# Norms between layers moved to VectorE in two halves with plain transposes, and a longer chunk-wise end of the feed-forward's last product

## The chip, the cores and the metric

The kernel runs on one core of a Trainium2 chip. The metric is the device time of one launch in microseconds (us). Each kernel is run several times; one execution is also recorded by the hardware profiler. The engines are named as in the profile: PE (TensorE, matrix products), PEld (its weight loads), DVE (VectorE), ACT (ScalarE), POOL (GpSimd) and SP (SyncE, which issues the weight transfers).

## The reference, cut to what matters

A block with adaptive norms, a Fourier and windowed-attention mixer and a mixture of experts is followed by a two-layer model. All tensors are float32, the sequence has 512 tokens and the width is 1024. The second model:

```python
def rms_norm(x, g):
    y = xf * lax.rsqrt(jnp.mean(xf * xf, axis=-1, keepdims=True) + NORM_EPS)
    return y * g

def conv_ffn(h, w_up, conv_w, conv_b, w_down):      # widths 1024 -> 2*2816 -> 1024
    u = causal_dwconv(h @ w_up, conv_w, conv_b)
    gate, up = jnp.split(u, 2, axis=-1)
    return (jax.nn.silu(gate) * up) @ w_down

x = first_block(...)                                 # phases A and B
for i in range(2):
    h = rms_norm(x, pre_g[i])                        # i = 0: even mixer, phase C
    h = mixer(h, ...)                                # i = 1: odd mixer, phase E
    x = x + rms_norm(h, post_g[i])
    h = conv_ffn(rms_norm(x, ffn_pre_g[i]), ...)     # phases D and F
    x = x + rms_norm(h, ffn_post_g[i])
```

So there are four norms of the whole x between layers: before C, before D, before E and before F.

## The kernel before, in words

The 512 tokens are four chunks of 128 rows; x stays in SBUF as four tiles of 128 x 1024. A product needs its left side transposed (hT, eight blocks of 128 columns of the width by 512 tokens). To keep float32 accuracy every operand is split into a high and a low part, and each product is three matmuls (mm3, lines 381 to 385: hi*hi, hi*lo, lo*hi). Weights arrive as float32 pieces through SP (L344), ACT casts the high part (L373), DVE subtracts to get the low part (L374); the two parts lie in rings of three buffers each (pool wp).

Phases run in the order A (first mixer), B (experts), C (even mixer), D (feed-forward 0), E (odd mixer), F (feed-forward 1). Each transition has the same steps, chunk by chunk. The last product of a phase is run by proj_m: with tail = n, the weight pieces of the last n*step blocks are held back and then used chunk by chunk, so that chunk 0 is finished early; evac takes a finished chunk from PSUM, and with a lag of one chunk post_norm (L456 to L460) adds the normed result to x, and the norm for the next phase follows. In feed-forward phases evac adds to osb (L1727), sums the squares on ACT (L414) and multiplies by the post gain on POOL (L1729); tail is 2 for the second half of the width of the last product. Blocks are counted by 128 of the inner width, 11 for this product, and step is 2; so with tail 2 the last two weight pieces (three blocks) are used chunk by chunk.

The norm (normer, L443 to L454) of one chunk: POOL multiplies x by the gain (L449, 128x1024), ACT sums squares (L414), ACT and DVE form the reciprocal root (rstd, L391 to L405), DVE writes a 128x128 diagonal of it (L452), and PE multiplies each of eight 128x128 blocks of the result by that diagonal, which transposes and scales at once (L438). ACT and DVE split each group of four blocks out of PSUM into the high and low part of hT (L388, L389). In B the scatter of the last two experts (L1172) and the add to x (L1175) are run chunk by chunk in front of the norm.

The order on each engine is made when the kernel is built: a scheduler takes instructions by their place in the program and by when their inputs are ready in its own model; an instruction that is pinned keeps its place. Within an engine the order is fixed at run time, so one that waits holds up those behind it. A row of gains (gain, L1249; row_load, L324) comes by a POOL-queue DMA that is pinned. In out_proj (L1437) the gain of the next norm is asked for before the post gain is loaded and scaled on POOL (L1441).

At the end of F no norm follows: store_chunk writes x out.

Of the kernel before, what the change touches and what calls it, by code (L numbers as in the profile page):

```python
# [9 lines left out]
F32 = mybir.dt.float32  # L10
# [5 lines left out]
OP = mybir.AluOpType  # L16
# [5 lines left out]
D = 1024  # L22
# [5 lines left out]
NF = DFF // 128  # L28
# [4 lines left out]
ROUTE = ((), (0,), (0, 1), (0, 1, 2, 3, 1, 2, 3, 2, 3))  # L33
SIDE = ()
NFIRST = 4
FILL = (0, 2, 2, 3, 3, 2, 2, 2, 0, 0, 0)
ODD = ("v0 v1 d0 d0 d0 d0 d0 d0 d0 d0 s0 d1 s0 d1 s0 d1 d0 d1 d1 s0 d1 s1 s0 d1 d1 s1 d1 s1 s1 s1").split()

# [24 lines left out]
def weight_chunks(phase):  # L63
# [6 lines left out]
    if phase == "A":  # L70
# [12 lines left out]
        for h in range(2):  # L83
            add("q", 2048, lambda z, h=h: _m(z["w_in"][0][:, qcols], 4 * h, 4, 0, 512))
            if h == 0:
                ada(3)
                ada(1)
            fill(FILL[h])
        add("kv", 2048, lambda z: _m(z["w_in"][0], 0, 8, 1024, 256))
        fill(FILL[2])  # L90
        for j in range(2):
            add("u", 2048, lambda z, j=j: _s(z["w_in"][0], slice(j * 256, j * 256 + 256)))
            fill(FILL[3 + j])
        for i in range(4):
            fill(FILL[5 + i])
        orow = np.array(list(range(512)) + [512 + (kv * 4 + r) * 64 + d for r in range(4) for kv in range(2)
                                            for d in range(64)])
        for half in range(2):
            for h in range(2):
                add("o", 2048, lambda z, h=h, half=half: _m(z["w_out"][0][orow], 4 * h, 4, half * 512, 512))  # L100
                if half:
                    fill(FILL[9 + h])
    if phase == "B":
# [160 lines left out]
class Kernel:  # L264
# [160 lines left out]
        nc.vector.scalar_tensor_tensor(out, xg, r, shift, op0=OP.mult, op1=OP.add)  # L425
        return out

    def transpose_split(self, rows, c, hT, bank=None, diag=None):

        nc = self.nc  # L430
        for g in range(2):
            pt = (bank or self.av)()
            for k in range(4):
                kk = 4 * g + k
                if diag is None:
                    nc.tensor.transpose(pt[:, k * 128:(k + 1) * 128], rows[:, kk * 128:(kk + 1) * 128], self.ident)
                else:
                    nc.tensor.matmul(pt[:, k * 128:(k + 1) * 128], rows[:, kk * 128:(kk + 1) * 128], diag,  # L438
                                     start=True, stop=True)
            dst = [h[:, 4 * g:4 * g + 4, c * 128:(c + 1) * 128] for h in hT]  # L440
            self.split(dst[0], dst[1], pt.rearrange("p (k t) -> p k t", k=4))

    def normer(self, gain, hT, bank=None):  # L443

        nc = self.nc

        def norm(c):
            xg = self.nrm.tile([128, D], F32, name="xn", tag="xn")
            nc.gpsimd.tensor_tensor(xg, self.x[:, c], gain, op=OP.mult)  # L449
            r = self.rstd(self.ssq(self.x[:, c]), 1, D)  # L450
            diag = self.sp.tile([128, 128], F32, name="diag", bufs=2)
            nc.vector.tensor_scalar(diag, self.ident, r, -0.5, op0=OP.mult, op1=OP.mult)  # L452
            self.transpose_split(xg, c, hT, bank, diag)
        return norm  # L454

    def post_norm(self, c, og, s0, s1):  # L456
# [549 lines left out]
    def phase_b(self, er, ep, after):  # L1006
# [5 lines left out]
        for i in range(2 + NRAW):  # L1012
            if i == 2 + NFIRST:
                self.pin(nc.sync.dma_start(self.hd[384:], self.last))
            ins = self.fetch(self.pos + i, *((self.wp, 2) if i < 2 else (pc, NRAW)))
            if i >= 2 + NFIRST:
                self.pin(ins)
# [660 lines left out]
    def phase_ffn(self, l, hT, after):  # L1678
        nc, tc, sp = self.nc, self.tc, self.sp
        with ExitStack() as es:  # L1680
            p = self.pool(es, "f_p")
            post = self.row_load(p, "ffn_post", D, l * D)
            nc.gpsimd.tensor_scalar(post, post, -0.5, None, op0=OP.mult)
            os_ = p.tile([128, 4, D], F32, name="osb")
            aT = self.pair_tile(p, "aT", 11)

            def gated(j, pss):
                u = []
# [15 lines left out]
            for si, (a, b) in enumerate(SEGS):  # L1704
                for j in range(a, b):
                    ws = self.pieces("up", 128)
                    if j == 0:
                        pss = [self.mm(), self.mm()]
                        self.proj_first(hT, list(ws), pss)
                    else:  # L1710
                        pss = []
                        for w in ws:
                            pss.append(self.mm())
                            self.proj_s(hT, w, pss[-1])
                    gated(j, pss)
                if si:
                    self.table()
                    nxt = after(p)
                for half in range(2):
                    sl = slice(half * 512, half * 512 + 512)  # L1720

                    def evac(c, ps):
                        o = os_[:, c, sl]
                        if si == 0:
                            nc.scalar.copy(o, ps)
                            return
                        nc.vector.tensor_tensor(o, o, ps, op=OP.add)  # L1727
                        s = self.ssq(o)
                        nc.gpsimd.tensor_tensor(o, o, post[:, sl], op=OP.mult)  # L1729
                        if half == 0:  # L1730
                            first[c] = self.half_sum(s)
                        else:
                            return lambda: (self.post_norm(c, os_[:, c], first[c], s), nxt(c))
                    self.proj_m(aT, "down", 3, 11, 512, evac, banks=[self.av] * 2 + [self.tp] * 2, tail=2 * half * si)

    def store_chunk(self, c):
        self.nc.sync.dma_start(self.out[c * 128:(c + 1) * 128], self.x[:, c])
# [53 lines left out]
```

## Time and profile before

| what | value |
|---|---|
| median of 3 runs | 2146.18 us (2145.84 to 2146.59) |
| the profiled execution's own time | 2144.74 us |
| its span, first to last instruction | 2143.0 us |
| PE busy | 2019.7 us (94%) |
| DVE busy | 1365.0 us (64%) |
| ACT busy | 1054.7 us (49%) |
| POOL busy | 186.5 us (9%) |
| mean granted TensorE clock | 0.980 |

Busy shares are averages over phases. What the change touches lies in five short stretches: around 857 to 880 us (B to C), 1109 to 1137 (C to D), 1490 to 1523 (D to E), 1742 to 1770 (E to F) and the last 20 us. In such a stretch the idle time of PE and the instruction that ends it tell more than the shares. [...]

### The profile page before, as it was taken

To read this page: it belongs to the slowest core of one execution; us is meant where nothing else is said; L and a number is where in the kernel's file an instruction comes from. 1 tells how busy PE (TensorE), PEld (TensorE's weight loads), DVE (VectorE), ACT (ScalarE), POOL (GpSimd) and SP (SyncE) were. 2 spreads that over 40 slices of the span, in tenths; PEclk is the share of its full clock that TensorE was granted. 3 is DMA by queue.
4 is the path that set the end of the run, shared out by engine and by line. 5 is a ranking of instruction groups with operands and counts; after the bars stand their busy time and mean duration, and the time that the engine had idled before them with its cause. 6 is when DMAs were issued, how large, how long until landed. Compare 5 with 4: busy or idle time off the path is not lost.

```text
span 2143.0 us, 25155 instructions
## 1 busy us (share of the span) xinstructions
PE 2019.7 (94%) x9459; PEld 1576.9 (74%) x9459; DVE 1365.0 (64%) x2304; ACT 1054.7 (49%) x1826; POOL 186.5 (9%) x166
## 2 busy tenths in 40 slices
PE   6899789999999999999999999999999999999997
PEld 5667667766666666877778888887887778888886
DVE  7675579988888888627755533553436766534553
ACT  3344277767676776426644433443325554423432
POOL 2103400000000000300011000002200030000002
PEclk8899889999999999999999999999999999999999
DMA  7744669999999995320122222222321022222221
GB/s 285 203 156 174 281 214 365 387 341 345 351 339 343 345 356 211 102 89 30 40 79 99 99 88 99 98 90 79 110 89 60 24 85 99 99 89 98 99 83 65
DMA packets 53933, 358.32 MB, mean 167 GB/s; under 512 B 6694, under 2 KB 7262, under 8 KB 14004
## 3 DMA queue, kind: packets, MB, share of 16 engines
q1 hardware_dynamic: 48148, 338.60, 42.6%
q0 software_dynamic: 5664, 18.12, 3.2%
q8 instruction: 74, 1.21, 0.2%
q14 instruction: 47, 0.39, 0.1%
HBM read 353.28 MB, written 4.46 MB: 167 GB/s over the span
## 4 chain that ended last, share of the span: by engine, by line
PE 83%; DVE 10%; ACT 3%; DMA 2%; issue 2%; POOL 0%; SPq 0%; DVEq 0%; ACTq 0%; POOLq 0%
PE mm L1098 14%; PE mm L384 13%; PE mm L383 13%; PE mm L385 13%; PE mm L1095 4%; DVE wlo L374 3%; PE tp L1128 2%; PE av L1172 2%; PE av L385 2%; PE av L383 2%; PE av L384 2%; PE tp L383 2%; PE tp L385 2%; PE tp L384 2%; PE mm L1223 1%
## 5 line engine op out<-in xcount | busy, mean ns | idle before, releaser
L374 DVE TENSOR_TENSOR wlo<-wraw,whi 128x1024 fp32r<-128x1024 f32 (+1 forms) x545 | 648.5, 1216 | 470.2 <-ACT whi L373 469.5
L373 ACT CAST whi<-wraw 128x1024 fp32r<-128x1024 f32 (+1 forms) x545 | 548.8, 1044 | 415.0 <-PE mm L384 151.9
L383 PE MATMUL mm<-hT_hi,whi 128*128 128x512 f32 (+1 forms) x960 | 374.8, 392 | 4.7 <-ACT whi L373 4.5
L384 PE MATMUL mm<-hT_lo,whi 128*128 128x512 f32 (+1 forms) x960 | 374.5, 390 | 2.2 <-DVE hT_lo L389 2.2
L385 PE MATMUL mm<-hT_hi,wlo 128*128 128x512 f32 (+1 forms) x960 | 373.4, 389 | 0.0
L383 PEld LDWEIGHTS mm<-hT_hi,whi 128*128 128x128 f32 x960 | 181.0, 189 | 47.2 <-ACT whi L373 5.3
L384 PEld LDWEIGHTS mm<-hT_lo,whi 128*128 128x128 f32 x960 | 181.2, 189 | 43.6 <-DVE hT_lo L389 3.0
L385 PEld LDWEIGHTS mm<-hT_hi,wlo 128*128 128x128 f32 x960 | 181.0, 189 | 40.8
L1098 PE MATMUL mm<-wlo,xs 128*128 128x512 f32 x448 | 164.1, 418 | 7.7 <-DVE wlo L374 7.6
L1098 PE MATMUL mm<-whi,xs 128*128 128x512 f32 x448 | 170.0, 428 | 0.4 <-ACT whi L373 0.4
L383 PE MATMUL mm<-whi,hT_hi 128*128 128x512 f32 (+2 forms) x288 | 110.6, 386 | 0.0
L384 PE MATMUL mm<-wlo,hT_hi 128*128 128x512 f32 (+2 forms) x288 | 110.1, 383 | 0.3 <-DVE wlo L374 0.3
L385 PE MATMUL mm<-whi,hT_lo 128*128 128x512 f32 (+2 forms) x288 | 109.2, 381 | 0.0
L1098 PEld LDWEIGHTS mm<-wlo,xs 128*128 128x128 f32 x448 | 77.7, 190 | 42.0 <-DVE wlo L374 28.4
L1098 PEld LDWEIGHTS mm<-whi,xs 128*128 128x128 f32 x448 | 83.4, 190 | 26.5 <-issue 8.4
L1172 PE MATMUL av<-y,ph 128*128 128x512 f32 x256 | 84.9, 427 | 14.1 <-ACT y L388 11.3
L1729 POOL TENSOR_TENSOR osb<-osb,row_ffn_post 128x512 f32<-128x512 f32 x16 | 25.4, 1599 | 708.8 <-ACT junk L414 379.1
L388 ACT CAST aT_hi<-cv 128x512 fp32r<-128x512 f32 x44 | 27.3, 621 | 118.9 <-DVE cv L1700 117.0
L1098 PE MATMUL mm<-wlo,act 128*128 128x512 f32 x224 | 81.0, 424 | 3.7 <-DVE wlo L374 3.6
L1098 PE MATMUL mm<-whi,act 128*128 128x512 f32 x224 | 81.7, 427 | 0.0
L1172 PEld LDWEIGHTS av<-y,ph 128*128 128x128 f32 x256 | 48.6, 192 | 40.9 <-ACT y L388 21.7
L1699 ACT ACTIVATE cv<-cv 128x512 f32<-128x512 f32 x44 | 27.8, 633 | 89.6 <-DVE cv L1696 89.6
(484 smaller groups left out, 3414.8 us busy)
## 6 DMA issues: line engine op xcount, KB each, us to landing
wraw<-in_wts SPq DMA_DIRECT2D x310, 1024.0 KB, 5.5
wraw<-in_wts SPq DMA_DIRECT2D x8, 768.0 KB, 4.3
x<-in_x SPq DMA_DIRECT2D x4, 512.0 KB, 11.1
out<-x SPq DMA_DIRECT2D x4, 512.0 KB, 2.6
wraw<-in_wts SPq DMA_DIRECT2D x2, 832.0 KB, 6.2
bias<-t5scr POOLq DMA_DIRECT2D x8, 192.0 KB, 15.8
hd<-xn POOLq DMA_DIRECT2D x3, 512.0 KB, 3.6
mod<-md POOLq DMA_DIRECT2D x1, 1024.0 KB, 11.0
```

What stands on the lines that cost most here:

```text
L373: i1 = nc.scalar.copy(hi[:, :n], t[:, a:a + n])
L374: i2 = nc.vector.tensor_tensor(lo[:, :n], t[:, a:a + n], hi[:, :n].bitcast(F32), op=OP.subtract)
L383: mm(ps, a[0], b[0], start=start, stop=False)
L384: mm(ps, a[0], b[1], start=False, stop=False)
L385: mm(ps, a[1], b[0], start=False, stop=stop)
L388: self.nc.scalar.copy(hi, src)
L1095: nc.tensor.matmul(ps[half], full[:, WHOLE.index(k)], w[:, sl], start=(k == 0), stop=(k == 7))
L1098: nc.tensor.matmul(ps[half], stat[:, k], w[q][:, 0, sl], start=(k + q == 0), stop=(k == 7 and q == 1))
L1128: nc.tensor.matmul(pt[:, k * 128:(k + 1) * 128], src[:, f * 128:(f + 1) * 128], dup, start=True, stop=True)
L1172: nc.tensor.matmul(ps, ph[:, c * 128:(c + 1) * 128], y[:, q, sl], start=(n == 1), stop=(n == 2 * len(es)))
L1699: nc.scalar.activation(u[0], u[0], AF.Silu)
L1729: nc.gpsimd.tensor_tensor(o, o, post[:, sl], op=OP.mult)
```

## The change: what it does, and the diff

In normer the gain row is multiplied by -0.5 once (on POOL); a chunk's norm then has, for each half of the width, one DVE instruction x * r * gain of 128x512, and four plain transposes on PE against the constant identity, and the split. The POOL product, the diagonal and the products with it are gone. In the feed-forward phases the tail constant of the last product's second half goes from 2 to 4 (seven of its eleven blocks are run chunk by chunk, from four held pieces), the weight parts of these phases go round five buffers instead of three (two more of each in the phase's own pool), and the post gain of the second half is multiplied on DVE.

```diff
--- before.py
+++ after.py
@@ -33,6 +33,7 @@
 ROUTE = ((), (0,), (0, 1), (0, 1, 2, 3, 1, 2, 3, 2, 3))
 SIDE = ()
 NFIRST = 4
+TAIL = 4
 FILL = (0, 2, 2, 3, 3, 2, 2, 2, 0, 0, 0)
 ODD = ("v0 v1 d0 d0 d0 d0 d0 d0 d0 d0 s0 d1 s0 d1 s0 d1 d0 d1 d1 s0 d1 s1 s0 d1 d1 s1 d1 s1 s1 s1").split()
 
@@ -425,32 +426,28 @@
         nc.vector.scalar_tensor_tensor(out, xg, r, shift, op0=OP.mult, op1=OP.add)
         return out
 
-    def transpose_split(self, rows, c, hT, bank=None, diag=None):
+    def transpose_split(self, rows, c, hT, g, bank=None):
 
         nc = self.nc
-        for g in range(2):
-            pt = (bank or self.av)()
-            for k in range(4):
-                kk = 4 * g + k
-                if diag is None:
-                    nc.tensor.transpose(pt[:, k * 128:(k + 1) * 128], rows[:, kk * 128:(kk + 1) * 128], self.ident)
-                else:
-                    nc.tensor.matmul(pt[:, k * 128:(k + 1) * 128], rows[:, kk * 128:(kk + 1) * 128], diag,
-                                     start=True, stop=True)
-            dst = [h[:, 4 * g:4 * g + 4, c * 128:(c + 1) * 128] for h in hT]
-            self.split(dst[0], dst[1], pt.rearrange("p (k t) -> p k t", k=4))
+        pt = (bank or self.av)()
+        for k in range(4):
+            kk = 4 * g + k
+            nc.tensor.transpose(pt[:, k * 128:(k + 1) * 128], rows[:, kk * 128:(kk + 1) * 128], self.ident)
+        dst = [h[:, 4 * g:4 * g + 4, c * 128:(c + 1) * 128] for h in hT]
+        self.split(dst[0], dst[1], pt.rearrange("p (k t) -> p k t", k=4))
 
     def normer(self, gain, hT, bank=None):
 
         nc = self.nc
+        nc.gpsimd.tensor_scalar(gain, gain, -0.5, None, op0=OP.mult)
 
         def norm(c):
+            r = self.rstd(self.ssq(self.x[:, c]), 1, D)
             xg = self.nrm.tile([128, D], F32, name="xn", tag="xn")
-            nc.gpsimd.tensor_tensor(xg, self.x[:, c], gain, op=OP.mult)
-            r = self.rstd(self.ssq(self.x[:, c]), 1, D)
-            diag = self.sp.tile([128, 128], F32, name="diag", bufs=2)
-            nc.vector.tensor_scalar(diag, self.ident, r, -0.5, op0=OP.mult, op1=OP.mult)
-            self.transpose_split(xg, c, hT, bank, diag)
+            for g in range(2):
+                sl = slice(g * 512, g * 512 + 512)
+                nc.vector.scalar_tensor_tensor(xg[:, sl], self.x[:, c, sl], r, gain[:, sl], op0=OP.mult, op1=OP.mult)
+                self.transpose_split(xg, c, hT, g, bank)
         return norm
 
     def post_norm(self, c, og, s0, s1):
@@ -1683,6 +1680,7 @@
             nc.gpsimd.tensor_scalar(post, post, -0.5, None, op0=OP.mult)
             os_ = p.tile([128, 4, D], F32, name="osb")
             aT = self.pair_tile(p, "aT", 11)
+            self.parts = (([(self.wp, 3)] * 3 + [(p, 2)] * 2) * 14)[:2 * NF + 24]
 
             def gated(j, pss):
                 u = []
@@ -1726,12 +1724,12 @@
                             return
                         nc.vector.tensor_tensor(o, o, ps, op=OP.add)
                         s = self.ssq(o)
-                        nc.gpsimd.tensor_tensor(o, o, post[:, sl], op=OP.mult)
+                        (nc.vector if half else nc.gpsimd).tensor_tensor(o, o, post[:, sl], op=OP.mult)
                         if half == 0:
                             first[c] = self.half_sum(s)
                         else:
                             return lambda: (self.post_norm(c, os_[:, c], first[c], s), nxt(c))
-                    self.proj_m(aT, "down", 3, 11, 512, evac, banks=[self.av] * 2 + [self.tp] * 2, tail=2 * half * si)
+                    self.proj_m(aT, "down", 3, 11, 512, evac, banks=[self.av] * 2 + [self.tp] * 2, tail=TAIL * half * si)
 
     def store_chunk(self, c):
         self.nc.sync.dma_start(self.out[c * 128:(c + 1) * 128], self.x[:, c])
```

## Rows read from the trace of the kernel before

**Rows 1.** Page of the profile: chain of work that ended last, shares by engine.

```profile
PE 83%; DVE 10%; ACT 3%; DMA 2%; issue 2%; POOL 0%; SPq 0%; DVEq 0%; ACTq 0%; POOLq 0%
```

**Rows 2.** Windows: stretch, length, busy us (instructions) by engine, clock, DMA share, GB/s.

```profile
857.00:877.00 20.00, 17.03 (x91) 13.74 (x90) 17.17 (x38) 9.88 (x24) 13.48 (x9) 0.91 0.27 78
977.00:1003.00 26.00, 25.99 (x153) 20.06 (x152) 19.75 (x89) 18.55 (x58) 0.54 (x1) 1.00 0.05 11
1109.00:1137.00 28.00, 23.52 (x176) 21.34 (x175) 18.78 (x41) 14.45 (x33) 11.49 (x7) 1.00 0.22 71
1140.00:1490.00 350.00, 350.00 (x1498) 281.52 (x1497) 168.90 (x198) 130.44 (x171) 5.95 (x4) 1.00 0.27 94
1490.00:1500.00 10.00, 5.90 (x26) 4.42 (x24) 7.91 (x13) 6.16 (x16) 7.92 (x4) 0.94 0.05 7
1500.00:1510.00 10.00, 8.46 (x38) 7.44 (x39) 7.61 (x16) 3.61 (x10) 3.69 (x2) 0.72 0.25 101
1742.00:1770.00 28.00, 23.54 (x167) 21.70 (x166) 17.49 (x39) 14.13 (x32) 10.80 (x6) 0.94 0.16 57
```

**Rows 3.** Timeline of PE at boundaries: start, length, instructions, idle before and its releaser.

```profile
865.27 0.50 PE L1172 MATMUL av<-y,ph 128*128 128x512 f32 x1 [1.96 <-DVE x L1175]
...
1128.54 2.02 PE L438 MATMUL av<-diag,xn 128*128 128x128 f32 x16 [1.81 <-DVE diag L452]
...
1500.57 3.76 PE L438 MATMUL av<-diag,xn 128*128 128x128 f32 x16 [4.67 <-DVE diag L452]
...
1508.98 2.02 PE L438 MATMUL av<-diag,xn 128*128 128x128 f32 x16 [0.97 <-DVE rs_y L404]
...
1761.39 3.51 PE L438 MATMUL av<-diag,xn 128*128 128x128 f32 x16 [1.83 <-DVE diag L452]
```

**Rows 4.** Groups by form, 1195 to 2143 us: count, busy us, mean ns, idle before.

```profile
L438 PE MATMUL av<-diag,xn 128*128 128x128 f32 x128 | 19.4, 315 | 9.0 <-DVE diag L452 8.0 <-DVE rs_y L404 1.0
...
L1641 PE MATMUL tp<-ident,s 128*128 128x128 f32 x32 | 4.5, 274 | 0.0
...
L452 DVE TENSOR_SCALAR diag<-ident,rs_y 128x128 f32<-128x128 f32 x8 | 2.4, 294 | 0.1
...
L1700 DVE TENSOR_TENSOR cv<-cv,cv 128x512 f32<-128x512 f32 x39 | 27.0, 692 | 1.4
```

**Rows 5.** Timeline of DVE: instructions beside POOL work, and the same ones without.

```profile
862.21 2.41 DVE L404 SCALAR_TENSOR_TENSOR rs_y<-rs_t,rs_y 128x1 f32<-128x1 f32 x1
...
1498.70 1.21 DVE L400 SCALAR_TENSOR_TENSOR rs_t<-rs_y,rs_v 128x1 f32<-128x1 f32 x1
...
1501.48 0.21 DVE L400 SCALAR_TENSOR_TENSOR rs_t<-rs_y,rs_v 128x1 f32<-128x1 f32 x1
...
1530.05 1.23 DVE L374 TENSOR_TENSOR wlo<-wraw,whi 128x1024 fp32r<-128x1024 f32 x1 [3.91 <-ACT whi L373]
...
1729.41 2.06 DVE L374 TENSOR_TENSOR wlo<-wraw,whi 128x1024 fp32r<-128x1024 f32 x1 [0.38 <-ACT whi L373]
```

**Rows 6.** Timelines of POOL and DVE where POOL scales a row of gains.

```profile
871.56 0.54 POOL L327 DMA_DIRECT2D row_lq<-in_rows  x1 [0.88 <-ACT hT_hi L388]
...
875.46 1.23 POOL L1274 TENSOR_SCALAR row_cq<-row_cq 128x384 f32<-128x384 f32 x1
...
1729.36 2.77 POOL L1441 TENSOR_SCALAR row_od_post<-row_od_post 128x1024 f32<-128x1024 f32 x1 [4.49 <-DMA row_od_post<-in_rows]
...
1732.16 1.89 DVE L1449 TENSOR_TENSOR osb<-mm,row_od_post 128x512 f32<-128x512 f32 x3 [0.69 <-POOL row_od_post L1441]
```

**Rows 7.** Timelines of PE, DVE and POOL at the kernel's end.

```profile
2129.68 0.40 PE L385 MATMUL tp<-whi,aT_lo 128*128 128x512 f32 x1
...
2132.39 0.68 DVE L1727 TENSOR_TENSOR osb<-osb,tp 128x512 f32<-128x512 f32 x1
...
2136.53 1.28 DVE L460 SCALAR_TENSOR_TENSOR x<-osb,rs_y,x 128x1024 f32<-128x1024 f32 x1
...
2133.89 2.32 POOL L1729 TENSOR_TENSOR osb<-osb,row_ffn_post 128x512 f32<-128x512 f32 x1 [2.51 <-ACT junk L414]
```

## The prediction

> **What bounds the kernel now.** I read the page's chain first: TensorE carries 83% of it, VectorE 10% [rows 1]. So a microsecond is won where TensorE works less or waits less. Then I asked for windows, to see where it waits. In the body of a feed-forward phase it is busy 350 of 350 us at full clock, in the stretch 1140 to 1490 [rows 2] (phase F looks the same). Nothing done to casts or buffers there can bring anything. The boundaries are different: idle time of TensorE is 2.97 us at B to C (20 less 17.03), 4.48 at C to D, 4.10 and 1.54 in the two stretches of D to E, 4.46 at E to F [rows 2]. The granted clock falls with it: 0.91, 1.00, 0.94 and 0.72, 0.94. Third, the timeline of TensorE at these places says who ends the wait [rows 3]: nearly always the norm (diag, rs_y), once, at B to C, the add to x. Fourth, the timeline of VectorE shows small instructions that last 2.41 and 1.21 us where 0.21 is usual, each beside a POOL product [rows 5]. Last, the end: after its last product the kernel runs a chain of VectorE, ScalarE and POOL [rows 7].
>
> **The change part by part.** The profiled execution took 2144.74 us (span 2143.0 and 1.74 around it), 1.44 under the median of the runs, 2146.18. Gains are worked out in its timeline and taken off the median.
>
> *Plain transposes.* A chunk's norm now issues 16 records on TensorE for its eight products with the diagonal, 2.02 us at full clock [rows 3]; a product of two plain float32 operands counts twice. The attention phases do the same 128x128 transposes against the identity with one record each, 32 in 4.5 us, 0.14 each [rows 4]; eight are 1.13. That is 0.89 us less per chunk, 3.6 per boundary, 14.2 for sixteen chunks. It is worth that only where TensorE is the limit.
>
> *Two halves on VectorE.* The diagonal (0.29) goes and two instructions of 128x512 with two SBUF inputs come; the nearest row is 0.69 [rows 4]. So VectorE has 1.09 more per chunk, and it no longer shares time with the POOL product: up to 1.0 back per chunk (1.21 against 0.21 [rows 5]). The chain from the reciprocal root to the first transposed half was 0.29 and half of 2.02, 1.30; it becomes 0.69 and half of 1.13, 1.25. To the second half it was 2.31 and becomes 1.94. So the chain of a chunk is between 0 and 0.4 shorter.
>
> *C to D and E to F.* There the last wait is for the norm (1.81 and 1.83 before the fourth chunk [rows 3]), which stands behind ScalarE's sum of squares and VectorE's splits. The shorter TensorE work turns into idle time, the chain gains up to 0.4 per chunk (1.5 in all), the heavier VectorE queue may lose as much. I take 0 for each, bounds 1.5 either way.
>
> *B to C.* The wait of 1.96 for x [rows 3] comes from a VectorE instruction of 2.41 beside POOL [rows 5]; without it 2.0 are won. TensorE could save 3.6 more, but VectorE is busy 17.17 of 20 here [rows 2] and gets 4.4 more, against 2.2 and 1.0 of blocked time that go. Bounds: 5.6 won to 1 lost. I take 2.5, near the one wait that has a row.
>
> *D to E, the longer chunk-wise end.* Now the last product runs three of eleven blocks by chunks, so the chunks end close together, and TensorE has nothing before the first norm: 4.67 idle, then the sixteen records take 3.76 where 2.02 is full speed [rows 3], because the clock has fallen (0.72 in that stretch [rows 2], a mixture of the two levels). Lost are 5.6 idle and 1.7 to 2.8 (0.28 of 10 us) of clock, about 8. With seven blocks a chunk takes 7/3 as long, chunk 0 is evacuated, added to x and normed beside the products of chunks 2 and 3, and the first products of E can follow. What is late next is the weights: three of the four held pieces lie in the wp ring from which E takes its first; the first of these is free only nine matmuls before the product's end, and its cast and subtraction (1.23 [rows 5] and about as much on ScalarE) stand then among the evacuations. I leave 1.5 of the 8 lost (bounds 0 and the old idle of 5.6): 6.5 won. Here TensorE is the limit afterwards, so the 3.6 of the transposes count too.
>
> *The end of F.* Chunk 3's add starts at 2132.39, though its product ended at 2130.08, because VectorE is held by a product of an earlier chunk that waits for POOL; then POOL multiplies by the gain for 2.32, and the last addition ends at 2137.81 [rows 7]. With 0.69 on VectorE in the place of 2.32, and the other chunks long done, the addition to x could start about 2.6 after the add and end about 3.9 after it, at 2134.0. That is 3.8 won; I take 3.5 (bounds 2 and 3.8) for semaphores. In D the same move is inside the 6.5.
>
> *The gains scaled on POOL.* Four instructions of 2.77 [rows 6] are new. Before E and before the feed-forward they can land in stretches where POOL is idle; beside one, a subtraction took 2.06 in place of 1.23 [rows 5], so 0.8 on VectorE each. Before E it lies in D's body, whose TensorE is busy throughout: 0. For B and C together I take 0.5 (bounds 0 and 1.7). At E to F the post gain is scaled at 1729.36, right when its load has landed, and VectorE waits 0.69 for it already [rows 6]; the new instruction stands in front, partly in the 4.49 in which POOL is idle. I take 1 lost (bounds 0 and 2.8). If the post gain's load were queued behind it, it would be 2.77 and 4.49, 7.3. Against this: the scheduler has put other loads ahead of a waiting scaling, row_lq's at 871.56 before row_cq's scaling at 875.46 [rows 6], though the program has them the other way.
>
> [...]
>
> *Five buffers in D and F* change nothing in bodies that are busy throughout; without them the four held pieces could not be held.
>
> **Sum.** 6.5 + 3.6 (D to E) + 2.5 (B to C) + 0 + 0 + 3.5 (end) - 0.5 - 1 = 14.6. From the median: 2131.6 us (2130.1 on the profiled execution's scale).
>
> **Rivals.**
> 1. *TensorE is the limit at every boundary.* Then all 14.2 of the transposes count, the whole 8, the 2.0 at B to C and 3.8 at the end, less 1.5 for the gains: 26.5, 2119.7. For it: TensorE's share of the chain. Against: the waits in rows 3 are for the norm.
> 2. *E starves behind the held pieces.* The stall before E stays and only its place changes: 6.5 goes, 8.1 is left, 2138.1. For it: the ring above. Against: chunk 0 and 1 are normed before the pieces are needed.
> 3. *VectorE becomes the limit at B to C, C to D and E to F.* Twelve chunks by 1.09 are 13.1, with no time given back by POOL; then 6.5 + 3.6 + 2.0 + 3.5 - 1.5 - 13.1 = 1.0, 2145.2: no change. For it: 17.17 of 20 busy; against: 18.78 and 17.49 of 28 [rows 2].
> 4. *Slower: the clock stays down through a boundary.* TensorE's work there is 17.0 + 23.5 + 14.4 + 23.5, 78 us, of which the old norm products are 32; the other 46 would take 46 more at the lower level, of which about 12 lie in time now idle. That is 34 against 14.6: 2165.6. It makes the kernel slower once over 0.58 of that work (26.6 of 46) runs at the lower level. For it: the fall at D to E and E to F (3.51 for 2.02 [rows 3]) with less idle before. Against: it recovered within a chunk each time, and a stretch of the attention that mixes such transposes with products was granted 1.00 throughout (977 to 1003 [rows 2]).
>  [...]
>
> **How the numbers follow.** Chances: forecast 0.55, rival 1 0.10, rival 2 0.20, rival 3 0.08, rival 4 0.07. The range for eight in ten goes from 2124 (the bounds of B to C, D to E and the two VectorE boundaries all on the good side reach 2122; most of rival 1 is left out) to 2141 (rival 2 with 2.8 lost on the gains). A change of 0.2%, 4.3 us, is about the least that a measurement of this kernel can tell. Forecast and rivals 1 and 2 are faster: 0.85; rival 3 is the same: 0.08; rival 4 slower: 0.07.
>
> **What would show it.** Right: sixteen norms with eight transposes of 0.14 each; no idle time over 2 us on TensorE before the first norm of E, and a clock near 1.00 from 1490 to 1510; no VectorE instruction of one column over 1 us at B to C; about 4 us from the last matmul to the last addition to x; windows of C to D and E to F as long as before. Wrong: E's first matmul waiting for whi or wlo; VectorE waits for POOL's scaling of row_od_post of several us; a clock under 0.9 in a boundary where it was 1.00.

## The result and the profile after

The changed kernel took 2123.76 us (median of 4 runs, 2122.05 to 2127.86) against 2146.39 for the kernel before in the same series (2145.84 to 2148.51). The ratio is 0.9897, with a 95% interval of [0.9885, 0.9908]: 22.6 us faster, where 14.6 were forecast. The median lies 0.2 us below the lower end of the range. The profiled execution took 2122.88 us (span 2121.1), 21.9 less than that of before.

The page of the changed kernel: busy time by engine, and the shares of the chain that ended last, which answer to [rows 1].

```profile
PE 2006.7 (95%) x9331; PEld 1563.3 (74%) x9331; DVE 1377.4 (65%) x2328; ACT 1055.5 (50%) x1826; POOL 151.0 (7%) x146
...
PE 82%; DVE 8%; issue 5%; ACT 3%; DMA 2%; POOL 0%; SPq 0%; DVEq 0%; POOLq 0%; ACTq 0%
```

Windows of the changed kernel at the boundaries (columns as in [rows 2]). They are B to C, C to D, three stretches of D to E, and E to F.

```profile
857.00:877.00 20.00, 19.35 (x93) 15.62 (x93) 18.44 (x42) 11.42 (x26) 7.68 (x9) 0.91 0.29 93
1104.00:1132.00 28.00, 21.02 (x138) 18.18 (x137) 24.24 (x44) 16.18 (x34) 7.48 (x4) 0.88 0.31 107
1485.00:1495.00 10.00, 9.43 (x42) 6.77 (x40) 8.96 (x15) 6.96 (x15) 3.97 (x8) 1.00 0.25 48
1495.00:1505.00 10.00, 9.16 (x44) 6.72 (x45) 9.13 (x21) 5.76 (x14) 2.44 (x5) 1.00 0.74 229
1505.00:1515.00 10.00, 10.00 (x48) 7.92 (x47) 5.70 (x9) 4.23 (x5) 0.00 (x0) 1.00 0.17 54
1727.00:1755.00 28.00, 21.95 (x137) 19.13 (x136) 22.72 (x45) 16.01 (x37) 0.00 (x0) 0.88 0.18 63
```

B to C went from 17.03 to 19.35 busy of 20 on TensorE. D to E lost both its idle time and its low clock (0.94 and 0.72 before, 1.00 now). C to D and E to F went the other way: TensorE is idle for 7.0 and 6.1 us of 28 (4.5 in both before), and the granted clock is 0.88 in both, where it was 1.00 and 0.94. The fall at C to D is one that the prediction had named as a sign of being wrong.

The timeline of PE in the changed kernel shows why (idle time and releaser in brackets, as in [rows 3]). One row is from B to C, two from C to D, two from D to E, one from E to F.

```profile
870.10 1.03 PE L435 MATMUL tp<-ident,xn 128*128 128x128 f32 x8
...
1112.91 1.09 PE L435 MATMUL av<-ident,xn 128*128 128x128 f32 x4 [4.92 <-DVE xn L449]
...
1124.85 1.29 PE L435 MATMUL av<-ident,xn 128*128 128x128 f32 x8 [1.18 <-DVE xn L449]
...
1484.63 0.66 PE L435 MATMUL av<-ident,xn 128*128 128x128 f32 x4
...
1496.07 0.60 PE L435 MATMUL av<-ident,xn 128*128 128x128 f32 x4
...
1736.51 1.94 PE L435 MATMUL av<-ident,xn 128*128 128x128 f32 x8 [4.91 <-DVE xn L449]
```

Eight transposes take 1.03 us back to back, near the 1.13 of the prediction. At D to E none of the groups waits. At C to D and E to F the second chunk's transposes now wait 4.9 for VectorE, and the clock falls inside that wait (0.50 granted from 1112 to 1118 us and from 1737 to 1742): four transposes take 1.09 there and 0.60 elsewhere.

Groups by form of the changed kernel, 1195 to 2121 us, which answer to [rows 4]:

```profile
L435 PE MATMUL av<-ident,xn 128*128 128x128 f32 x64 | 10.4, 295 | 6.0 <-DVE xn L449 5.9
...
L449 DVE SCALAR_TENSOR_TENSOR xn<-x,rs_y,row_od_pre 128x512 f32<-128x512 f32 x8 | 5.6, 747 | 0.0
```

The end, timelines of PE and DVE in the changed kernel, which answer to [rows 7]:

```profile
2112.88 0.40 PE L386 MATMUL tp<-whi,aT_lo 128*128 128x512 f32 x1
...
2113.31 0.69 DVE L1725 TENSOR_TENSOR osb<-osb,tp 128x512 f32<-128x512 f32 x1 [0.67 <-PE tp L386]
2114.79 0.69 DVE L1727 TENSOR_TENSOR osb<-osb,row_ffn_post 128x512 f32<-128x512 f32 x1 [0.79 <-ACT junk L415]
...
2116.22 1.28 DVE L457 SCALAR_TENSOR_TENSOR x<-osb,rs_y,x 128x1024 f32<-128x1024 f32 x1
```

TensorE ends at 2113.28, so the last addition ends 4.2 after it (7.7 before).

### The profile page after: what moved, and what is told of

It reads as the page before. It is cut to its first block, busy times and chain, and to the rows that moved or that the text cites. A ratio compares the mean times of both kernels' runs of the same rounds, so it can differ in the third digit from the quotient of the medians.

```text
span 2121.1 us, 24893 instructions
## 1 busy us (share of the span) xinstructions
PE 2006.7 (95%) x9331; PEld 1563.3 (74%) x9331; DVE 1377.4 (65%) x2328; ACT 1055.5 (50%) x1826; POOL 151.0 (7%) x146
## 4 chain that ended last, share of the span: by engine, by line
PE 82%; DVE 8%; issue 5%; ACT 3%; DMA 2%; POOL 0%; SPq 0%; DVEq 0%; POOLq 0%; ACTq 0%
PE mm L1095 15%; PE mm L384 13%; PE mm L385 13%; PE mm L386 13%; PE mm L1092 4%; PE tp L1125 2%; DVE wlo L375 2%; PE av L1169 2%; PE av L386 2%; PE av L384 2%; PE av L385 2%; PE tp L386 2%; PE tp L385 2%; PE tp L384 2%; PE mm L1220 1%
## 5 line engine op out<-in xcount | busy, mean ns | idle before, releaser
L384 PE MATMUL av<-whi,aT_hi 128*128 128x512 f32 x176 | 69.3, 394 | 0.0
```

Of the source, the lines that this page charges most:

```text
L384: mm(ps, a[0], b[0], start=start, stop=False)
```

## The experiments

The theory from these rows: B to C is worth 6.4, because POOL left the norm and the transposes are shorter; D to E 9.4; the end 3.5 and 1.6 more after the last addition; the two feed-forward bodies 1.6 each. The rivals were that one part alone does it all, and that five buffers speed the bodies. The stretch up to the last expert of B changes from run to run (54.6 to 78.5 us of it at the low clock, 0.50, in the profiled runs, and an end between 1.3 earlier and 6.7 later than in the kernel before). So I compare stages between the same instructions in each trace. Differences to the kernel before in us, minus is shorter:

| stage | changed | norms_only | ffn_end_only | buffers_only | two_records | pool_product | post_pool | parts_shifted | no_gain_scaling | a0 | opt_f | fold_a0 |
|---|---|---|---|---|---|---|---|---|---|---|---|---|
| B to C | -6.4 | -6.5 | -0.4 | 0.0 | -2.8 | -0.8 | -6.5 | -6.5 | -6.2 | -8.2 | -7.0 | -6.1 |
| C to D | 0.8 | 1.0 | 4.9 | 5.0 | 3.0 | 2.7 | 0.9 | 0.9 | 0.7 | 1.1 | 3.5 | 1.0 |
| body of D | -1.6 | 0.0 | -1.7 | -1.6 | -1.9 | -1.9 | -1.6 | -0.4 | -3.6 | -3.6 | -7.1 | -7.3 |
| D to E | -9.4 | -2.4 | -7.3 | -0.3 | -8.2 | -8.0 | -7.9 | -9.2 | -5.1 | -9.4 | -11.8 | -6.2 |
| E, E to F | 0.3 | -0.6 | 3.4 | 3.5 | 2.0 | 5.4 | 2.0 | 1.9 | -0.7 | 2.1 | 6.1 | -2.2 |
| body of F | -1.9 | 0.0 | -1.9 | -1.9 | -2.2 | -2.2 | -1.9 | -0.4 | -3.9 | -3.8 | -7.4 | -7.5 |
| last product to last addition | -3.5 | 0.0 | -3.5 | 0.0 | -3.5 | -3.5 | -3.3 | -3.5 | -3.5 | -3.5 | -3.5 | -3.5 |
| after it | -1.6 | 0.0 | -1.6 | 0.0 | -1.6 | -1.6 | 0.0 | -1.6 | -1.6 | -1.5 | -1.6 | -1.6 |

The markers are B's last expert (last VectorE product of it), the first out_proj result of C, the first 512-column product on hT in D and F, the first add of the last product's first half, and the first value copy of E. The row B to C holds C's attention too, and body of F runs to the last product. A difference of up to 1.7 in one cell can come from the clock alone: E in post_pool, parts_shifted and a0 has 3.4 us at the low level that the changed kernel's has not (a0: 0.94 granted from 1670 to 1700 us, the changed kernel 1.00), and 3.4 us at 0.50 are 1.7 us of work. The version a32 is not in the table; it lies within 0.3 of a0 in every row but B to C (-7.1).

**norms_only: the norm without the feed-forward's part.**

```diff
-TAIL = 4
+TAIL = 2
-            self.parts = (([(self.wp, 3)] * 3 + [(p, 2)] * 2) * 14)[:2 * NF + 24]
-                        (nc.vector if half else nc.gpsimd).tensor_tensor(o, o, post[:, sl], op=OP.mult)
+                        nc.gpsimd.tensor_tensor(o, o, post[:, sl], op=OP.mult)
```

> Kernel before with the new norm alone (one VectorE instruction per half, plain transposes, gain scaled on POOL); the feed-forward's tail stays 2, its parts three buffers, its post gain on POOL. Theory (B to C won about 6.4 from the norm, the transposes about 3.6 at D to E, C to D and E to F lose about 1, the bodies of D and F win only from buffers): about 9 won against the kernel before, 2137.4 us; the body of D (first 512-wide product of D to the first add of its last product) stays as long as before, 326.4 us. Rival 1 (the bodies win 1.6 each through the norm, for instance by what stands on the queues at their start): 12 won, 2134. Rival 2 (the norm is worth only the 2.5 forecast at B to C, since the stall before E stays and eats the transposes): 2 to 3 won, 2144.

Measured: 2139.28 us, ratio 0.9978 [0.9968, 0.9987]. The stages bear the theory out: 6.5 at B to C, 2.4 at D to E, bodies unchanged. The stages sum to 8.5; of these 4.7 (by the ratio) show in the whole time, and the stretch ahead of B's last expert, 3.3 later in this profile, is the likely rest.

**buffers_only: five buffers for the feed-forward's weights and nothing else** (the `self.parts` line added to the kernel before).

> Kernel before with five buffers in place of three for the weight parts of both feed-forward phases, nothing else. Theory: each body gains 1.6, so 3.2 won, 2143.2 us, with TensorE busy throughout in both. Rival (TensorE is busy throughout with three buffers already and its spacing does not depend on them): within 0.5 of the kernel before, 2146.4.

Measured: 2148.97, ratio 1.0022 [1.0012, 1.0033], slower. Both were wrong about the whole: each body did win 1.6 to 1.9, but with the old norm C to D lost 5.0 and E to F 3.5. The waits of PE at C to D in this kernel (who waits for whom: us in all, times, longest):

```profile
PE av L438 <- DVE diag L452: 6.0, 4, 4.5
```

Before it was 3.4 in all, 1.8 the longest. The timelines of DVE and PE in this kernel show what stands in front of the fourth chunk's norm:

```profile
1127.02 1.23 DVE L374 TENSOR_TENSOR wlo<-wraw,whi 128x1024 fp32r<-128x1024 f32 x1 [0.43 <-ACT whi L373]
...
1128.29 1.22 DVE L374 TENSOR_TENSOR wlo<-wraw,whi 128x1024 fp32r<-128x1024 f32 x1
...
1130.05 3.76 PE L438 MATMUL av<-diag,xn 128*128 128x128 f32 x16 [4.49 <-DVE diag L452]
```

With two more buffers free, VectorE subtracts two more weight pieces ahead of that norm. The wait grows by 2.7, and the sixteen records behind it take 3.76 where they took 2.02 [rows 3]: over 1109 to 1137 us the granted clock is 0.88 in this kernel, 1.00 in the kernel before. Together that is 4.4 of the 5.0.

**ffn_end_only: the feed-forward's part without the norm** (tail 4, five buffers, second half's gain on VectorE, in the kernel before).

> Kernel before with the feed-forward's part alone (tail 4, five buffers, second half's post gain on VectorE); the norm keeps POOL and the diagonal. Theory: 6.5 at D to E, 5 at the end (3.5 to the last addition and 1.6 after it), 3.2 in the bodies: 14.7 won, 2131.7 us; the first norm of E waits on TensorE under 2 us where it waited 4.67. Rival 1 (buffers do nothing to the bodies): 11.5 won, 2134.9. Rival 2 (with POOL's product in the norm, the chunk-wise end meets VectorE blocked by POOL and the stall before E stays): 5 to 8 won, 2140.

Measured: 2136.96, ratio 0.9957 [0.9945, 0.9970]. D to E wins 7.3 and the end 5.1, but the boundaries lose what they lose with the buffers alone (4.9 and 3.4). By their ratios the two halves of the change gain 4.7 and 9.2, 13.9 together, and 22.1 when they are made at once: the new norm takes away most of what the buffers cost (0.8 and 0.3 in the changed kernel). At C to D one reason is in the rows: over 1109 to 1137 us the granted clock is 0.88 in norms_only, in buffers_only and in the changed kernel alike, so the two halves pay together once for what each pays alone.

**two_records: transposes as float32 products with the identity.**

```diff
-            nc.tensor.transpose(pt[:, k * 128:(k + 1) * 128], rows[:, kk * 128:(kk + 1) * 128], self.ident)
+            nc.tensor.matmul(pt[:, k * 128:(k + 1) * 128], rows[:, kk * 128:(kk + 1) * 128], self.ident,
+                             start=True, stop=True)
```

> Changed kernel with the transposes as float32 products with the identity (two records each, 16 per chunk as before) and everything else as changed. Theory (TensorE is the limit at D to E, 3.6, and the norm work of B to C is worth most of its 3.6; at C to D and E to F VectorE is): 5 to 8 slower than the changed kernel, 2130 us. Rival 1 (what was won at the boundaries is POOL leaving the norm, and the shorter transposes turn into idle time): within 1.5 of the changed kernel, 2124. Rival 2 (TensorE is the limit at all four): 14 slower, 2138.

Measured: 2132.50, ratio 0.9939 [0.9923, 0.9955], some 9 slower than the changed kernel. The total is near the theory, its places are not: against the changed kernel 3.6 at B to C, 2.1 at C to D, 1.1 at D to E, 1.7 at E to F.

**pool_product: POOL back in the norm, plain transposes kept.**

```diff
+            nc.gpsimd.tensor_tensor(xg, self.x[:, c], gain, op=OP.mult)
             for g in range(2):
                 sl = slice(g * 512, g * 512 + 512)
-                nc.vector.scalar_tensor_tensor(xg[:, sl], self.x[:, c, sl], r, gain[:, sl], op0=OP.mult, op1=OP.mult)
+                nc.vector.tensor_scalar(xg[:, sl], xg[:, sl], r, None, op0=OP.mult)
```

> Changed kernel with POOL back in the norm: POOL multiplies x by the gain (128x1024), VectorE multiplies the halves by the reciprocal root in place of the three-operand instruction; plain transposes stay. Theory (of the 6.4 won at B to C 3.6 are the shorter transposes and 2.8 POOL's absence): the two stages of B to C lose 2.8, C to D and E to F lose 0 to 1.5 each, about 4 slower than the changed kernel, 2128 us. Rival (POOL's absence is worth nothing, its product lies beside the sum of squares, and the two-operand instructions are shorter than 0.75): no loss at B to C, 1 to 2 won at C to D and E to F each, 2121.

Measured, one run: 2137.66, some 14 slower than the changed kernel. B to C gives back 5.7 of its 6.4, E and E to F 5.1, C to D 1.9, D to E 1.3. The theory was right in kind and far too small. The timelines of DVE and POOL in this kernel, at B to C:

```profile
865.60 2.40 DVE L405 SCALAR_TENSOR_TENSOR rs_y<-rs_t,rs_y 128x1 f32<-128x1 f32 x1
```

```profile
865.57 2.41 POOL L447 TENSOR_TENSOR xn<-x,row_ev_pre 128x1024 f32<-128x1024 f32 x1 [0.88 <-issue]
```

A one-column instruction of VectorE that takes 0.16 alone (the median of its 53 executions) starts with POOL's product and ends with it. It is a step of the next norm, so the whole chain stands. The two contributions at B to C overlap: without the short transposes 3.6 are lost, without POOL's absence 5.7, and there were 6.4 in all.

**post_pool: the second half's post gain back on POOL, tail 4 kept.**

```diff
-                        (nc.vector if half else nc.gpsimd).tensor_tensor(o, o, post[:, sl], op=OP.mult)
+                        nc.gpsimd.tensor_tensor(o, o, post[:, sl], op=OP.mult)
```

> Changed kernel with the second half's post gain back on POOL; tail 4 and five buffers stay. Theory (POOL's 2.32 product was in the chain of the end): from TensorE's last product to the last addition the time goes back by the full 3.5, to about 7.7; the 1.6 after the last addition stays won, since it comes from chunks 0 to 2 being stored earlier; D to E loses 1 to 2 of its 9.4. About 5 slower, 2129 us. Rival (the chunk-wise end does it: with the other chunks long done VectorE does not wait for POOL): under 2.4 back, the length of the one POOL product.

Measured, one run: 2129.04. The theory fell at the end: from the last product to the last addition only 0.2 comes back, and it is the 1.6 after the addition that is lost. POOL's timeline there:

```profile
2114.39 1.29 POOL L1727 TENSOR_TENSOR osb<-osb,row_ffn_post 128x512 f32<-128x512 f32 x1 [3.58 <-ACT junk L415]
2119.25 1.26 POOL L1727 TENSOR_TENSOR osb<-osb,row_ffn_post 128x512 f32<-128x512 f32 x1 [3.58 <-ACT junk L415]
```

POOL's product took 2.32 in the kernel before [rows 7], beside VectorE's addition for the chunk before. Two such additions, timeline of DVE in the kernel before:

```profile
2130.16 2.30 DVE L460 SCALAR_TENSOR_TENSOR x<-osb,rs_y,x 128x1024 f32<-128x1024 f32 x1
...
2133.81 1.28 DVE L460 SCALAR_TENSOR_TENSOR x<-osb,rs_y,x 128x1024 f32<-128x1024 f32 x1
```

The first ran beside an earlier product of POOL (1.26 from 2130.12), the second beside the product of 2.32. With seven blocks by chunks each chunk is alone, the product takes 1.26 and lies beside the reciprocal root. So with tail 4 in place the engine is worth 0.2 before the last addition, and the chunk-wise end has won the other 3.3. What the engine alone would be worth with tail 2 no run shows. D to E loses 1.5, as expected.

**no_gain_scaling: the factor -0.5 folded into the reciprocal root** (the four POOL scalings go, no instruction comes into the norms). Some of the lines that differ; the two constants are new one-column tiles.

```diff
-        nc.gpsimd.tensor_scalar(gain, gain, -0.5, None, op0=OP.mult)
+        nc.vector.tensor_scalar(v, ssq, -4.0 / D, self.eps4, op0=OP.mult, op1=OP.add)
+        nc.scalar.activation(y, y, AF.Exp, scale=-0.5, bias=self.lnh)
+        nc.vector.scalar_tensor_tensor(y, t, 3.0, y, op0=OP.add, op1=OP.mult)
```

> Changed kernel without the four scalings of the gain row on POOL: the factor -0.5 is folded into the reciprocal root (Exp with a bias of ln 0.5, v times -4, 3 in place of -3, the same number of instructions). Theory (the scalings cost about 1 at B to C, 1 at C to D, 1.1 to 2 at E to F): about 3 faster than the changed kernel, 2120.8 us. Rival (they lie beside work that VectorE has time for, and what they delay is given back by the next wait): within 1 of the changed kernel, 2123.8.

Measured: 2122.58, ratio 0.9896 [0.9880, 0.9912], the same as the changed kernel. That is no sign of a free scaling: E and E to F win 1.0, the bodies win 2.0 each, which no theory had, and D to E loses 4.3. There this kernel's order of VectorE differs, TensorE waits for weights, and the granted clock is 0.83 from 1485 to 1505 us (1.00 in the changed kernel):

```profile
PE mm L389 <- DVE wlo L379: 3.3, 1, 3.3
```

**parts_shifted, a32, a0: where the tiles lie.** The bodies were busy throughout before and after; what changed is the pace. In the built programs hT, aT and yT lie at 32 modulo 64 bytes and wp's ring at 0; the two extra buffers lie at 32. In no_gain_scaling, with its two small constants, hT, aT, yT and wp's ring lie 64 bytes further on. Each kernel is the changed one with unused tiles of 32 bytes:

```diff
 parts_shifted, behind aT:
+            p.tile([128, 1], F32, name="padp")
 a32, in cst behind col and in sp:
+        self.cst.tile([128, 1], F32, name="pad")
+        self.sp.tile([128, 1], F32, name="pads", bufs=1)
 a0, in sp and ahead of the first pool on the right:
+        self.sp.tile([128, 1], F32, name="pads", bufs=1)
+        k.pool(ctx, "padr", side="right").tile([128, 1], F32, name="padr")
```

> Changed kernel with one unused tile of 32 bytes in the feed-forward's pool, ahead of its two extra buffers: these move by 32 bytes, five buffers stay five. Theory (a 512-column product takes about 233.5 ns where its moving rows and the weights lie 32 bytes apart modulo 64 and 231.2 where they lie alike; the extra buffers win 1.6 us per body only because they happen to lie as hT does): the bodies of D and F go back to 234.0 ns per product, 1.6 each, 3.2 slower than the changed kernel, 2127 us. Rival (the number of buffers does it): 232.9 ns and the time of the changed kernel, 2123.8.

> Changed kernel with two unused tiles of 32 bytes, so that the weights' ring of the wp pool lies as hT, aT and yT do, 32 modulo 64. Theory (the distance modulo 64 sets the pace): 1825 products at 233.1 and 1836 at 234.0 fall to 231.2 or less, 8.6 us, up to 16 if they fall to 229.2: 2108 to 2115 us; bodies of D and F at 231.2 or less per product. Rival (addresses do nothing): 2123.8, 232.9 ns.

> Changed kernel with unused tiles of 32 bytes so that wp's ring stays at 0 modulo 64 and hT, aT, yT and the rest come to 0 as well. Theory (only the distance counts): the same as with all at 32, 2108 to 2115 us. Rival 1 (what counts is that both lie at 0 modulo 64): clearly faster than that version, by 5 or more. Rival 2 (addresses do nothing): 2123.8.

Measured: parts_shifted 2125.26, ratio 0.9913 [0.9898, 0.9927]; a32 2121.37, 0.9884 [0.9866, 0.9903]; a0 2119.51, 0.9878 [0.9861, 0.9896]. One window of 300 us inside the body of D tells the pace: how many products (x) are in it, TensorE busy throughout and at full clock. Before, changed, parts_shifted, a0 (columns: stretch, length, PE busy and count, clock, DMA share, GB/s):

```profile
1150.00:1450.00 300.00, 300.00 (x1283) 1.00 0.26 92
```

```profile
1150.00:1450.00 300.00, 300.00 (x1290) 1.00 0.26 94
```

```profile
1150.00:1450.00 300.00, 300.00 (x1285) 1.00 0.27 95
```

```profile
1150.00:1450.00 300.00, 300.00 (x1298) 1.00 0.27 95
```

That is 233.8, 232.6, 233.5 and 231.1 ns per product (from start to start 0.2 to 0.4 more, since products that only reach into the window are counted: 234.0, 232.9, 233.7 and 231.5). Moving the extra buffers by 32 bytes takes back most of what they won (1.2 of 1.6 per body): the place did most of it, not the number. With all tiles alike modulo 64 the bodies win 1.9 more each. The rival "addresses do nothing" falls, and "0 is better than 32" too: a32 has 1297 in the same window. The size fell short: 3.9 in the bodies, where 8.6 to 16 were expected over the whole kernel. In a0 E and E to F are 1.8 longer than in the changed kernel, with 3.4 us more at the low clock in this profile.

**opt_f and fold_a0: a version that beats both.** opt_f takes the addresses and the folding, runs the second half of C's last product wholly by chunks, and puts the extra buffers first in their cycle; fold_a0 takes the addresses and the folding alone.

```diff
 opt_f alone:
-            self.proj_m(yT, name, chunks, tot, 512, evac, tail=2 * half)
+            self.proj_m(yT, name, chunks, tot, 512, evac, tail=2 * chunks * half)
+            self.parts = [(self.wp, 3)] * 4 + [(p, 2)] * 2 + [(self.wp, 3)] * 2   # where chunks == 2
-            self.parts = (([(self.wp, 3)] * 3 + [(p, 2)] * 2) * 14)[:2 * NF + 24]
+            self.parts = (([(p, 2)] * 2 + [(self.wp, 3)] * 3) * 14)[:2 * NF + 24]
```

> Changed kernel with four things more: all large tiles at 0 modulo 64 bytes; the factor -0.5 folded into the reciprocal root, no scalings of the gain row; the second half of C's last product wholly by chunks (eight blocks, two more buffers), so that a chunk takes 5.6 us of TensorE in place of 2.8; in D and F the two extra buffers come first in the cycle of five. Theory (at C to D VectorE is the limit because chunks end faster than its 5 us per chunk): the 4.9 us wait for the second chunk's norm goes, C to D wins 3 to 5; bodies of D and F 231.5 ns per product (2 each); the wait for the post gain at E's end 1.3: 2110 to 2115 us. Rival (VectorE's work per boundary is the limit wherever the chunks end): C to D as in the changed kernel, 2118 to 2120 from the addresses alone.

> Changed kernel with two things of the version before it (label opt_f): all large tiles at 0 modulo 64 bytes and the factor -0.5 folded into the reciprocal root; C's last product and the cycle of the five buffers as in the changed kernel. Theory (the pace of 228.9 ns in opt_f's bodies comes from where its tiles lie, 64 bytes further than in a0; its losses at C to D and E to F come from the buffers' new cycle and C's longer end, which put the first products behind the norms): bodies at about 229 ns, 5.5 us shorter each than in the changed kernel; C to D and E to F stay within 1 of the changed kernel, with 6.8 us of low clock each; 1.3 won at the end of E: 2110 to 2113 us. Rival 1 (the pace came from the buffers' cycle): bodies at 231.4 as in a0, 2118. Rival 2 (a faster body costs clock at the boundaries whatever the order): 229 ns, but C to D and E to F lose 3 to 5 each, 2118 to 2120.

Measured: opt_f 2118.98, ratio 0.9877 [0.9860, 0.9893]; fold_a0 2115.72, ratio 0.9860 [0.9837, 0.9882], the fastest, some 8 us below the changed kernel. Both lie above what was expected of them (2110 to 2115 and 2110 to 2113). opt_f missed its aim: C to D lost 2.7 more, and TensorE still waits 4.0 and 5.1 there for two of the norms. In the changed kernel and in fold_a0 a chunk's transposes and F's first products alternate; opt_f has nothing but transposes from 1732.87 to 1746.25, and the same at C to D from 1116.18 to 1124.78, and the clock falls for longer. Waits of PE at E to F in opt_f, and a window:

```profile
PE av L451 <- DVE xn L464: 12.2, 3, 4.3
```

```profile
1740.00:1750.00 10.00, 5.70 (x27) 5.37 (x26) 8.21 (x13) 5.30 (x10) 0.00 (x0) 0.50 0.05 11
```

fold_a0 keeps the pace and not these losses (C to D 1.0, as changed), so rivals 1 and 2 of its expectation fall. Which of the two, C's longer end or the buffers' new order, cost opt_f its losses, no run separates.

```profile
1150.00:1450.00 300.00, 300.00 (x1313) 1.00 0.27 95
```

228.5 ns per product, 7.3 us less per body than in the kernel before. It still waits 3.3 at D to E for weights, as no_gain_scaling does, so more is to be had.

## Why the prediction was right or wrong

The direction was right and the size fell short: 14.6 forecast, 22.6 measured, at the edge of the range. The stages of the changed kernel sum to 23.3. What was missing are B to C (3.9 more than forecast), the bodies (3.5, forecast at nothing) and the time after the last addition (1.6, not in the sum).

- **B to C: 2.5 forecast, 6.4 measured; this term failed most.** The step "TensorE could save 3.6 more, but VectorE is busy 17.17 of 20 here and gets 4.4 more" took busy time for work. Part of it was an instruction of 0.16 that took 2.41 beside POOL's product [rows 5]; with POOL gone TensorE became the limit (busy 19.35 of 20), and both the 2.0 of the wait and the 3.6 of the transposes counted (two_records: 3.6; pool_product: 5.7). The upper bound of 5.6 was the nearest, and 0.8 short.
- **Bodies: 0 forecast, 3.2 measured** (and 0.3 behind F's). "Five buffers change nothing in bodies that are busy throughout" is true of waits. But a busy engine can have a pace, and the pace of a product went from 233.8 to 232.6 ns, most of it by the place of the extra buffers (parts_shifted).
- **D to E: 10.1 forecast, 9.4 measured.** The longer end alone gave 7.3 (6.5 forecast), and none of the norms' transposes waits in the changed kernel. The 3.6 of the transposes was mis-sized: two_records puts them at 1.1 here, of the 2.1 that the new norm adds to the longer end. The wait for weights that was feared is 0.7 in all in the changed kernel, and 3.3 in the two folded ones without opt_f's order, so rival 2 was close.
- **C to D and E to F: 0 each forecast; 0.8 lost, and 0.3 lost with the scalings in it** (1 forecast for these; no_gain_scaling shows 1.0). The term's reason was right in part: the wait is for VectorE, but the shorter TensorE work did not simply turn into idle time, since two_records puts the shorter transposes at 2.1 and 1.7 here. VectorE's longer queue (4.9 us before the second chunk) and the lower clock take as much or more; the clock was in no term of the sum, and 0.88 over 28 us is up to 3.4 us of work.
- **The end: 3.5 forecast and measured, and that the size fits is luck.** I counted POOL's 2.32 against VectorE's 0.69; post_pool shows that with tail 4 this swap is worth 0.2, so the chunk-wise end won 3.3. I also read the late start of chunk 3's add wrongly: VectorE did not wait for POOL there, it was in an addition that took 2.30 instead of 1.28 beside POOL's product. The swap's own gain is the 1.6 after the last addition, which was not forecast.
- **The gains' scaling: 1.5 forecast in all, about 1 measured.** Beside two of the scalings a VectorE instruction took longer, shown by the timelines of POOL and DVE in the changed kernel. The first scaling below is the post gain's, which the kernel before has too; the second is new:

```profile
1112.23 3.16 POOL L1680 TENSOR_SCALAR row_ffn_post<-row_ffn_post 128x1024 f32<-128x1024 f32 x1 [3.60 <-DMA row_ffn_post<-in_rows]
...
1119.17 3.21 POOL L442 TENSOR_SCALAR row_od_pre<-row_od_pre 128x1024 f32<-128x1024 f32 x1 [3.25 <-DMA row_od_pre<-in_rows]
...
1112.01 2.19 DVE L449 SCALAR_TENSOR_TENSOR xn<-x,rs_y,row_ffn_pre 128x512 f32<-128x512 f32 x2
...
1119.66 2.06 DVE L457 SCALAR_TENSOR_TENSOR x<-osb,rs_y,x 128x1024 f32<-128x1024 f32 x1
```

  Undisturbed these take 1.41 and 1.28 (at 1104.18 and 1106.10), so 0.8 was lost each time, the estimate. Not every instruction lost it: at E to F a subtraction beside the new scaling took 1.22 (1714.18), and the same one 2.06 beside the post gain's in the kernel before [rows 5]. Beside a product of two tensors on POOL (2.41) in pool_product 2.2 was lost: an instruction of 0.16 took 2.40. At E to F the new scaling stands in front of the post gain's, as was feared: VectorE waits 2.7 for the post gain, 0.69 before [rows 6], and 0.7 in no_gain_scaling.

```profile
DVE osb L1446 <- POOL row_od_post L1438: 2.7, 1, 2.7
```

- **Rival 4, the clock.** It fell at C to D and E to F, 0.88 over 28 us in each, and at C to D of norms_only, two_records and fold_a0 too (0.88 over 28 us in each); at D to E it was 1.00 with the same transposes. The rows go with the idle time ahead of it: a wait of 4.9 us at each of the two where it fell, none over 0.6 at D to E. Two more rows say the same: it fell at C to D in buffers_only, which has the old norm and a wait of 4.5, and at D to E in no_gain_scaling and fold_a0 (0.83 and 0.91 from 1485 to 1505 us), which wait 3.3 there. How long a wait it takes these rows do not tell: in the kernel before one of 1.8 stands ahead of the fourth chunk at both C to D, with 1.00, and E to F, with 0.94 [rows 2, rows 3]. The rival counted work at the lower level twice, and the trace of the kernel before bears that out: the granted clock is 0.50 from 1499 to 1505 us. Its price of 34 us was far off, since each fall in the changed kernel cost at most 3.4 us of work (0.12 of 28).

## What to carry to other kernels

VectorE's busy time beside POOL's product was not its load (2.40 us for an instruction of 0.16): before an added instruction is charged to an engine, look for instructions that a neighbour stretched and subtract that. A stage in which an engine is busy throughout can still change its time (1283 products in 300 us before, 1313 in fold_a0), so count instructions per window before calling it fixed. And two halves of a change can each give less, or lose, alone (4.7 and 9.2 us here) and more together (22), so try them together before one is dropped.

## What the runs showed of the hardware that was not expected

- The pace of 512-column float32r products, start to start at full clock, changed with where the tiles lie: in the window of 300 us in D it is 232.6 ns in the changed kernel and 233.5 in parts_shifted, whose two extra buffers lie 32 bytes further (per product, by the counts of the window). Over the 512-column products of whole traces, those whose moving rows and weights lie 32 bytes apart modulo 64 took 233.1 to 234.1 ns in the kernel before, the changed one, norms_only and no_gain_scaling. Those that lie alike took 231.2 to 231.7 in the first three and 229.2 in no_gain_scaling. What sets it is not settled: in fold_a0 products that lie 64 bytes apart modulo 128 take 233.2 in one group and 229.1 in another, and in a0 products that lie alike modulo 128 take 232.9 in one group and 227.8 in another.
- The time after the last addition is 3.6 us where POOL does nothing near the end and 5.2 where it has a product there (before, norms_only, buffers_only, post_pool), though the last store is issued right after the addition in both. What lies in these 1.6 us no trace shows.
- POOL's own product took longer beside VectorE as well: 1.26 to 1.29 us for 128x512 in post_pool, 2.32 beside VectorE's addition in the kernel before.
